# Two more plain column blocks, later sums of squares, and a halved last down projection in a float32 encoder trunk

## The chip, the cores and the metric

The kernel runs on one core of one Trainium2 chip. The metric is the time of one execution on the device in microseconds (us), by the median of several runs. PE is TensorE, DVE is VectorE, ACT is ScalarE, POOL is GpSimd, SP is SyncE; PE's weight loads (PEld) run beside its products.

## The reference, cut to what matters

Two layers over x of 512 positions and 1024 channels, in float32. Each layer is attention with a residual addition, then a mixer; the change lies in the mixer:

```python
x = x + jnp.einsum('bsm,md->bsd', y, w_out[l])
h = rmsnorm(x, g_ffn[l])
gate, val = jnp.split(jnp.einsum('bsd,df->bsf', h, w_up[l]), 2, axis=-1)   # 1024 -> 2 x 2816
gate = centred_dwconv(gate, conv_w[l], conv_b[l])                           # width 3 over the positions
x = x + jnp.einsum('bsf,fd->bsd', jax.nn.silu(gate) * val, w_down[l])       # 2816 -> 1024
```

2816 hidden channels are 22 blocks of 128, 1024 channels are 8.

## The kernel before, in words

Everything is held transposed, channels on the partitions and the 512 positions along the free dimension. Every float32 operand is split into a rounded part (hi, by ACT) and a remainder (lo, by DVE), and a product is three PE instructions, hi x hi, hi x lo and lo x hi (`mm3`, L525). Weights come by SP's queue into `wr`, ACT rounds them to `wh`, DVE subtracts to `wl` (`w_load` L434, `w_high` L484, `w_low` L493); three such units can be ready ahead.

**The planner.** The program is written by tracks (Python generators) that offer one operation at a time; `Machine.run` (L261) models when each could start and, for each engine, takes the offer that starts first, or among offers within 0.1 us of it the one with the lowest rank (`RK`, L47). So the ranks and the model fix each engine's order when the program is built. Ranks that matter here: sums of weights 25, half sums of the input 22, weights 36 while a unit is ready ahead and 2 when none is, x additions behind the output projection 8, sums of squares `nsq` 6, additions of the mixer 42, the column chains 50 plus the block's number. All operations are recorded in one helper, so all have line L258 in the profile; the tiles' names tell them apart. PE's own order in the mixer is one track, `ffn` (L1528), which goes through `mixer_order` (L375).

**Into the mixer.** The last products of the output projection (`out_last`, L1202) are added to x by DVE, and for each of the 8 channel blocks ACT writes nf_h = x times the gain, DVE the remainder nf_l (`Norm.add`, L542). `squares` (L553) sums x squared over the blocks (ACT squares to nf_q, DVE adds to nf_sum), `rms` (L569) reduces that on PE to nf_ss and takes the power -1/2 on POOL, `rb_track` (L1229) spreads the result over the partitions (PE rps, ACT rb). The products of the plain columns don't need rb; what is done with their result does.

**Plain columns** (`up_step` L1370). A hidden block's gate and its value are 8 x 3 products of 512 columns each, each into its own PSUM bank, out of five (`FT`, L1367). `chain_f` (L1282) waits for rb, multiplies the gate by it (DVE, tile gp, which frees the bank), convolves (ACT and twice DVE), takes the SiLU (ACT), multiplies by rb (POOL) and by the value (DVE, cv<-cv,up, which frees the other bank); `act_out` splits the result (act, or acth and actl).

**Column pairs** (`pair_step` L1459, `up_pair` L1386). Two hidden blocks at once by Strassen's scheme with seven products of halves: 7 x 4 x 3 products of 256 columns for the two gates, as many for the two values. The input's half sums (`mixer_forms` L1308: ha, hb, hs, ht and the split f, fa, fb, fc) are made once per layer, when rb is there. The weights' sums ws are made for each pair by `w_sums` (L456), four operations that DVE or POOL may do (`either`). What the products give is put together in dp and du by ACT and DVE.

**Down.** `down_step` (L1548) adds a part's hidden blocks up in one bank per output block (3 products of 512 columns for each hidden block), `down_add` (L1565) adds that to x. Hidden blocks come in four parts:

```python
FF_PARTS = ((0, 6), (6, 12), (12, 18), (18, 22))
PLAIN = 4
```

The first four blocks are plain columns, the other 18 are nine pairs. Part 0's columns come first, then the eight down steps (one per output block) of each part, with the next part's columns spread among them. `later` (L1597) starts the next layer's norm behind the fifth step of the last part; in layer two the outputs are written as each output block is done. `_lay_out` (L1612) arranges the weights in memory.

Of the kernel before, what the change touches and what calls it, by code (L numbers as in the profile page):

```python
# [46 lines left out]
RK = {"w": (2, 45, 30), "qkb": (55, 18), "x": 33, "xl": 8, "a": 2, "b": 18, "evac": 49, "qka": 60, "kv": 45,  # L47
      "bn": 2, "nsq": 6, "av": -4, "bv": 4, "ch": 50, "add": 42, "sec": 1, "nxs": 42, "fin": 42, "sum": 25,
      "hf": 22, "wf": 36}
# [252 lines left out]
def kernel(  # L302
# [71 lines left out]

    def mixer_order():  # L375

        ups = [[(f, 1) for f in range(f0, min(f1, PLAIN))] + [(f, 2) for f in range(max(f0, PLAIN), f1, 2)]
               for f0, f1 in FF_PARTS]
        for f, n in ups[0]:
            yield "up", 0, f, n  # L380
        for pi in range(len(FF_PARTS)):
            after = ups[pi + 1] if pi + 1 < len(FF_PARTS) else []
            at = {NK * i // len(after): u for i, u in enumerate(after)}
            for d in range(NK):
                if d in at:
                    yield ("up", pi + 1, *at[d])
                yield "dn", pi, d, 0

    units = []
    for l in range(depth):  # L390
# [10 lines left out]
        for what, pi, f, n in mixer_order():  # L401
            if what == "dn":
                units.append((w_down[pi][l, f], (FF_PARTS[pi][1] - FF_PARTS[pi][0], P), "down"))
# [130 lines left out]
    class Norm:  # L534
# [18 lines left out]
        def squares(self):  # L553
            eng = dve
            for k in range(NK):
# [8 lines left out]
                yield act.activation(sq[:, :S], x_sb[k], AF.Square)  # L564
                yield eng.tensor_tensor(out=self.part, in0=self.part, in1=sq[:, :S], op=ALU.add)
                m.drop("tmp", sq)
# [98 lines left out]
    def layer(l, norm):  # L665
# [576 lines left out]

        BIG = ("keep", "pair")
        mix = {"forms": 14}

# [5 lines left out]
        def act_out(f, ct):  # L1251

            pi = [i for i, (f0, f1) in enumerate(FF_PARTS) if f0 <= f < f1][0]
            yield lambda: bool(act_places(pi))
# [11 lines left out]
            m.drop("tmp", ct)  # L1266
            m.flags.add(f"{lf}act{f}")

        def conv(f, gt, ct):
# [189 lines left out]
        def pair_step(f):  # L1459
# [34 lines left out]
            def value_piece(n, b, pt, ut, fl):  # L1494
# [25 lines left out]
                i = n // 2  # L1520
                if all(("v", q) in gate for q in (2 * i, 2 * i + 1)):
                    m.spawn(RK["ch"] + f, act_out(f + i, gate["cv", i]))
# [5 lines left out]
        def ffn():  # L1528
            steps = list(mixer_order())
            b_st["rb_left"] = PLAIN + 1  # L1530
# [4 lines left out]
            for i, (what, pi, f, n) in enumerate(steps):  # L1535
                if what == "dn":
                    yield from down_step(pi, f)
                elif n == 1:
                    yield from up_step(f)
                else:  # L1540
                    yield from pair_step(f)
# [6 lines left out]
        def down_step(pi, d):  # L1548
            f0, f1 = FF_PARTS[pi]
            m.flags.add(f"{lf}dn{pi}_{d}")  # L1550
# [7 lines left out]
            done_with(w)  # L1558
            m.spawn(RK["add"], down_add(d, tag, bank, acc, pi == len(FF_PARTS) - 1))
            if d == NK - 1:  # L1560
                for f in range(f0, f1):
                    for v in b_st.pop(("act", f))[0]:
                        m.drop(*v)

        def down_add(d, tag, bank, acc, last):  # L1565
            yield dve.tensor_tensor(out=x_sb[d], in0=x_sb[d], in1=acc, op=ALU.add)
            m.drop(tag, bank)
            if last:
                if l + 1 < depth:
                    yield from nxt.add(d)  # L1570
                else:
                    yield sync.dma_start(out_v[:, d], x_sb[d])

# [21 lines left out]
        if l + 1 < depth:  # L1595
            nxt = Norm(l + 1, 0, f"na{l + 1}")
            def later():  # L1597
                yield m.has(f"{lf}rb", f"{lf}dn{len(FF_PARTS) - 1}_{SQ_FROM}")
                m.spawn(RK["nxs"], nxt.squares())
                m.spawn(2, nxt.rms())  # L1600
# [11 lines left out]
def _lay_out(inp):  # L1612
# [24 lines left out]
    w = a["w_down"].reshape(L, NF, P, NK, P)  # L1637
    for i, (f0, f1) in enumerate(FF_PARTS):
        o[f"w_down{i}"] = np.ascontiguousarray(w[:, f0:f1].transpose(0, 3, 2, 1, 4))
    col = lambda v: v.reshape(L, -1, P).transpose(2, 0, 1)  # L1640
# [21 lines left out]
def _build(nc, arrays, depth=DEPTH):  # L1662
    ap = {n: nc.dram_tensor(n, v.shape, F32, kind="ExternalInput").ap() for n, v in arrays.items()}
    out = nc.dram_tensor("outT", (D, S), F32, kind="ExternalOutput").ap()
    with tile.TileContext(nc, schedule_with_timeline_sim=True) as tc:
        kernel(
            tc, ap["xT"], ap["w_first"], ap["w_in"], ap["w_out0"], ap["w_out1"], ap["w_up"],
            tuple(ap[f"w_down{i}"] for i in range(len(FF_PARTS))), ap["col_par"], ap["row_par"],
            ap["rope"], ap["mask"], ap["ident"], out, depth)
# [11 lines left out]
```

## Time and profile before

| | |
|---|---|
| median of 3 runs | 1184.47 us (1183.8 to 1187.16) |
| the profiled execution | 1185.19 us |
| its span, first to last instruction | 1183.1 us |
| mean granted clock of PE | 0.993 |
| busy: PE / PE weight loads / DVE / ACT / POOL | 1163.1 / 1053.0 / 981.9 / 663.2 / 202.3 us |
| moved by DMA | 103.12 MB |

A matmul's recorded length is longer than its share of PE, because products overlap: what a product costs is the distance of starts. DVE's and ACT's instructions overlap a little at their ends as well. Each of the 2 us stretches below shows how much of it an engine was busy and which clock was granted to PE (1.00 is 2.4 GHz, 0.50 is 1.2 GHz).

### The profile page before, as it was taken

The numbers are of one execution on the slowest core, as the hardware profiler recorded it, in microseconds if no ns is written. First come the engines' busy times: TensorE is split into PE (matmuls) and PEld (weight loads), VectorE is DVE, ScalarE is ACT, GpSimd is POOL, SyncE is SP. The second block draws the span as 40 slices with busy tenths as digits, with TensorE's granted clock in tenths as the row PEclk, the third lists the DMA queues.
The fourth block names the chain that finished last, engine by engine and source line by source line (L and its number), as shares of the span: only waits on it lengthen the run. The fifth ranks groups of instructions, "written<-read, shape, count | busy, mean of one in ns | idle before, by whom it ended". The sixth has DMA issues, their size and how long they took to land.

```text
span 1183.1 us, 20177 instructions
## 1 busy us (share of the span) xinstructions
PE 1163.1 (98%) x7796; PEld 1053.0 (89%) x7796; DVE 981.9 (83%) x1797; ACT 663.2 (56%) x1187; POOL 202.3 (17%) x254
## 2 busy tenths in 40 slices
PE   9999999999999999999999989999999999999998
PEld 7999888978999999999889989888789999999997
DVE  6988899779998888887659888898799988888863
ACT  6779766455564454444537876665555544544441
POOL 2433721010100000000042556110111000000000
PEclk9999999989999999999999999999899999999999
DMA  6221111123223322332332121111232223233323
GB/s 233 66 72 55 54 55 36 54 72 107 68 99 112 111 99 99 112 125 71 107 118 73 37 71 37 55 54 54 71 124 61 96 88 112 98 112 103 121 81 116
DMA packets 33343, 103.12 MB, mean 87 GB/s; under 512 B 3936, under 2 KB 4192, under 8 KB 33248
## 3 DMA queue, kind: packets, MB, share of 16 engines
q1 hardware_dynamic: 33248, 101.84, 26.0%
q8 instruction: 61, 1.00, 0.4%
q14 instruction: 34, 0.28, 0.1%
HBM read 99.73 MB, written 2.10 MB: 86 GB/s over the span
## 4 chain that ended last, share of the span: by engine, by line
PE 79%; DVE 13%; ACT 5%; issue 2%; POOL 0%; DMA 0%; SPq 0%; DVEq 0%; ACTq 0%
PE up L258 32%; PE dn L258 20%; PE wo L258 6%; PE pj_bk L258 3%; PE pj_bv L258 2%; PE pj_akq L258 2%; PE pj_bq L258 2%; DVE wl L258 2%; PE yb L258 2%; PE sc_b L258 2%; PE pt_a L258 1%; PE pv_a L258 1%; PE sc_a L258 1%; PE wt_b L258 1%; ACT so_a L258 1%
## 5 line engine op out<-in xcount | busy, mean ns | idle before, releaser
L258 ACT CAST wh<-wr 128x1024 fp32r<-128x1024 f32 (+2 forms) x200 | 177.2, 887 | 158.9 <-PE up L258 41.3
L258 DVE TENSOR_TENSOR wl<-wr,wh 128x1024 fp32r<-128x1024 f32 (+2 forms) x193 | 196.7, 1020 | 62.9 <-ACT wh L258 62.7
L258 ACT CAST wh<-ws 128x1024 fp32r<-128x1024 f32 x72 | 75.4, 1048 | 109.2 <-DVE ws L258 46.1
L258 PE MATMUL up<-fc,wh 128*128 128x256 f32 x576 | 106.4, 285 | 1.8 <-DVE du L258 1.8
L258 PE MATMUL up<-fa,wh 128*128 128x256 f32 x576 | 107.0, 283 | 0.0
L258 PE MATMUL up<-fb,wh 128*128 128x256 f32 x576 | 105.6, 284 | 0.0
L258 PEld LDWEIGHTS up<-fc,wh 128*128 128x128 f32 x576 | 89.4, 191 | 2.6 <-ACT cv L258 2.1
L258 PEld LDWEIGHTS up<-fb,wh 128*128 128x128 f32 x576 | 89.8, 192 | 0.4 <-ACT dp L258 0.2
L258 PEld LDWEIGHTS up<-fa,wh 128*128 128x128 f32 x576 | 89.8, 192 | 0.1
L258 DVE TENSOR_TENSOR wl<-ws,wh 128x1024 fp32r<-128x1024 f32 x72 | 89.5, 1245 | 0.4 <-ACT wh L258 0.2
L258 PE MATMUL dn<-act,wh 128*128 128x512 f32 x288 | 88.9, 390 | 0.0
L258 PE MATMUL up<-fa,wl 128*128 128x256 f32 x288 | 81.7, 284 | 0.0
L258 PE MATMUL up<-fb,wl 128*128 128x256 f32 x288 | 81.5, 283 | 0.0
L258 PE MATMUL up<-fc,wl 128*128 128x256 f32 x288 | 81.4, 283 | 0.0
L258 PE MATMUL dn<-acth,wh 128*128 128x512 f32 x208 | 81.0, 389 | 0.0
L258 PE MATMUL dn<-actl,wh 128*128 128x512 f32 x208 | 81.0, 389 | 0.0
L258 PE MATMUL dn<-acth,wl 128*128 128x512 f32 x208 | 80.9, 389 | 0.0
L258 POOL TENSOR_TENSOR du<-du 128x256 f32<-128x256 f32 x12 | 8.9, 742 | 395.9 <-DVE du L258 395.9
L258 DVE TENSOR_TENSOR x<-x,dn 128x512 f32<-128x512 f32 x64 | 43.7, 682 | 32.8 <-PE dn L258 32.8
L258 DVE SCALAR_TENSOR_TENSOR cv<-gp,cols,cv 128x512 f32<-128x512 f32 x88 | 63.9, 745 | 0.0
L258 PEld LDWEIGHTS dn<-act,wh 128*128 128x128 f32 x288 | 53.3, 188 | 10.4
L258 ACT ACTIVATE e_b<-sc_b,mx_b,rqb 128x512 f32<-128x512 f32 x64 | 49.1, 776 | 14.6 <-DVE mx_b L258 14.6
(269 smaller groups left out, 3452.4 us busy)
## 6 DMA issues: line engine op xcount, KB each, us to landing
wr<-w_up SPq DMA_DIRECT2D x88, 512.0 KB, 4.5
wr<-w_down SPq DMA_DIRECT2D x48, 384.0 KB, 3.1
wr<-w_in SPq DMA_DIRECT2D x28, 512.0 KB, 3.5
wr<-w_out SPq DMA_DIRECT2D x16, 512.0 KB, 3.4
wr<-w_down SPq DMA_DIRECT2D x16, 256.0 KB, 2.6
x<-xT SPq DMA_DIRECT2D x8, 256.0 KB, 5.5
prob_f<-w_first SPq DMA_DIRECT2D x8, 256.0 KB, 5.6
wr<-w_first SPq DMA_DIRECT2D x4, 512.0 KB, 3.6
```

The source lines that it names most:

```text
L258: getattr(self.raw[op.eng], op.name)(*op.args, **op.kw)
```

## The change

Six blocks instead of four are plain columns in both layers, so eight pairs are left. The rank of the sums of squares goes from 6 to 44. In layer two the parts are of 6, 6, 4 and 6 blocks, and the last part goes down two output blocks at a time by the same scheme of seven products of halves: the halves are of the positions, of two hidden blocks and of two output blocks. For it, `act_forms` makes four split tiles for each pair of hidden blocks in place of `act_out`, and `w_sums` and the casts treat the down weights as a pair's. The columns of that last part are spread over the first five of part 2's eight steps (`EARLY`).

```diff
-FF_PARTS = ((0, 6), (6, 12), (12, 18), (18, 22))
-PLAIN = 4
+FF_PARTS = (((0, 6), (6, 12), (12, 18), (18, 22)), ((0, 6), (6, 12), (12, 16), (16, 22)))
+HALVED = ((), (3,))
+EARLY = 5
+PLAIN = 6
...
-      "bn": 2, "nsq": 6, ...
+      "bn": 2, "nsq": 44, ...
...
+            n = NK // 2 if pi in HALVED[l] else NK
+            gap = min(n, EARLY) if pi + 1 in HALVED[l] else n
+            at = {gap * i // len(after): u for i, u in enumerate(after)}
+            for d in range(n):
                 if d in at:
                     yield ("up", pi + 1, *at[d])
-                yield "dn", pi, d, 0
+                yield "dp" if pi in HALVED[l] else "dn", pi, d, 0
...
+            if what == "dp":
+                units.append((tuple(w_down[l][pi][2 * f + i] for i in range(2)), (nf_part, P), "pair"))
+                units.extend([(None, (nf_part, P), "sum"), (None, (nf_part, P), "sum"), (None, (nf_part // 2, P), "rest")])
...
+        def act_forms(f, ct):
...
+            left, right, both = ce[:, LO], ce[:, HI], slice(0, S)
+            a = yield from place(f"fma{l}_{f}")
+            yield from split(a, left, LO, [("B11", LO)])
+            b = yield from place(f"fmb{l}_{f}")
+            yield from split(b, cf[:, both], both, [("B21", LO), ("B22", HI)])
+            yield either(cf[:, HI], cf[:, HI], right, ALU.subtract)
+            yield either(right, right, left, ALU.subtract)
+            yield either(left, cf[:, HI], left, ALU.add)
+            c = yield from place(f"fmc{l}_{f}")
+            yield from split(c, ce[:, both], both, [("T2", LO), ("T1", HI)])
+            yield either(cf[:, LO], cf[:, LO], left, ALU.subtract)
+            d = yield from place(f"fmd{l}_{f}")
+            yield from split(d, cf[:, both], both, [("T4", LO), ("T3", HI)])
...
+                if any(parts[p][0] <= f < parts[p][1] for p in HALVED[l]):
+                    if all(("v", q) in gate for q in range(4)):
+                        m.spawn(RK["ch"] + f, act_forms(f, [gate["cv", q] for q in range(2)]))
...
+        def down_pair(pi, p, last):
...
+            def add(b, x, o, d):
+                yield dve.tensor_tensor(out=x[:, o], in0=x[:, o], in1=b[2][:, LO], op=ALU.add)
...
+            def second(b):
+                yield dve.tensor_tensor(out=ut[:, 0], in0=pt[:, 0], in1=b[2][:, LO], op=ALU.add)
+                yield either(x1[:, HI], x1[:, HI], ut[:, 0], ALU.add)
+                yield either(both, both, ut[:, 0].unsqueeze(1).broadcast_to([P, 2, CW]), ALU.add)
...
+            def fourth(b):
+                yield dve.tensor_tensor(out=ut[:, 1], in0=pt[:, 1], in1=b[2][:, LO], op=ALU.add)
+                yield either(x2[:, HI], x2[:, HI], ut[:, 1], ALU.add)
...
+            yield from product(b0, u0, 0, "B11", True, True)
+            m.spawn(2, keep(b0, 0, "p1"))
+            yield from product(b1, u1, 0, "T1", True, True)
+            m.spawn(2, keep(b1, 1, "p5"))
+            yield from product(b0, u0, nh, "B21", False, True)
+            m.spawn(RK["add"], add(b0, x1, LO, 2 * p))
+            yield from product(b1, u1, nh, "B22", False, True)
+            m.spawn(RK["add"], add(b1, x1, HI, 2 * p))
+            yield from product(b3, u2, 0, "T3", True, True)
+            m.spawn(RK["sec"], fourth(b3))
+            yield from product(b2, u2, nh, "T2", True, True)
+            m.spawn(RK["sec"], second(b2))
+            yield from product(b3, u3, 0, "T4", False, True)
+            m.spawn(RK["add"], add(b3, x2, LO, 2 * p + 1))
```

`product` is as in `up_pair`, with the part's three block pairs in place of the input's four. An output block is written once its three additions are done.

## Rows read from the trace of the kernel before

**Rows 1.** The page of the profile: busy time of each engine with its share of the span and its instructions, and the granted clock of PE in 40 slices (tenths, 9 is 90% or more).

```profile
PE 1163.1 (98%) x7796; PEld 1053.0 (89%) x7796; DVE 981.9 (83%) x1797; ACT 663.2 (56%) x1187; POOL 202.3 (17%) x254
...
PEclk9999999989999999999999999999899999999999
```

**Rows 2.** The chain that ended last, in order of time: start in us, length in us, engine, tile, number of instructions. The first two lines are small groups of the attention stage, 252.55 and 839.45 stand behind the insertion of rps in each layer, the last two are a column pair and the end of layer two.

```profile
219.41 0.79 PE ss_yb L258 x8
222.35 0.89 PE rt_yb L258 x8
252.55 8.67 PE up L258 x38
...
839.45 8.67 PE up L258 x38
...
958.75 20.20 PE up L258 x168
...
1141.31 38.12 PE dn L258 x168
```

**Rows 3.** PE's timeline at the start of the mixer, layer one (233 to 250 us) and layer two (the last line): start, us, operation, output<-inputs, shapes, count, and in brackets the idle time before it with its releaser.

```profile
236.20 0.40 PE L258 MATMUL up<-nf_h,wh 128*128 128x512 f32 x1
...
239.81 0.50 PE L258 MATMUL up<-nf_l,wh 128*128 128x512 f32 x1 [0.30 <-DVE nf_l L258]
...
242.76 0.50 PE L258 MATMUL up<-nf_h,wh 128*128 128x512 f32 x1 [0.95 <-ACT nf_h L258]
...
823.03 0.40 PE L258 MATMUL up<-nf_h,wh 128*128 128x512 f32 x1
```

**Rows 4.** What PE waited for, from the last output products to the first column pair: 226 to 300 us (three lines) and, for nf_l in layer two, 812 to 890 us (the last line). Total us, times, longest.

```profile
PE up L258 <- DVE nf_l L258: 1.2, 4, 0.3
PE up L258 <- ACT nf_h L258: 1.0, 1, 1.0
PE up L258 <- DVE du L258: 0.9, 1, 0.9
...
PE up L258 <- DVE nf_l L258: 1.3, 4, 0.3
```

**Rows 5.** DVE's timeline in the same place, layer one; columns as in rows 3.

```profile
231.36 0.42 DVE L258 TENSOR_TENSOR x<-x,wo 128x256 f32<-128x256 f32 x1 [0.30 <-PE wo L258]
...
238.40 0.69 DVE L258 TENSOR_TENSOR nf_sum<-nf_sum,nf_q 128x512 f32<-128x512 f32 x1
239.00 0.75 DVE L258 SCALAR_TENSOR_TENSOR nf_l<-x,cols,nf_h 128x512 fp32r<-128x512 f32 x1
239.67 0.68 DVE L258 TENSOR_TENSOR nf_sum<-nf_sum,nf_q 128x512 f32<-128x512 f32 x1
...
241.53 0.41 DVE L258 TENSOR_TENSOR x<-x,wo 128x256 f32<-128x256 f32 x1
```

**Rows 6.** Table of stretches of 2 us, layer one: length, busy time of each engine with its instructions, then PE's granted clock, share and rate of the DMA engines.

```profile
242.00:244.00 2.00, 0.90 (x3) 0.54 (x4) 2.00 (x4) 2.00 (x4) 0.00 (x0) 1.00 0.00 0
...
246.00:248.00 2.00, 2.00 (x10) 1.92 (x9) 0.93 (x3) 0.78 (x1) 0.14 (x1) 0.50 0.25 39
...
250.00:252.00 2.00, 2.00 (x9) 1.61 (x9) 0.00 (x0) 0.00 (x0) 0.00 (x0) 0.61 0.67 250
```

**Rows 7.** DVE's timeline further on: the mean square from PE (nf_v), the first use of rb (ha), and the reads that give PSUM banks back (gp is a gate, cv<-cv,up a value).

```profile
247.62 0.16 DVE L258 TENSOR_SCALAR nf_v<-nf_ss 128x4 f32<-128x4 f32 x1 [1.07 <-PE nf_ss L258]
...
253.26 0.75 DVE L258 SCALAR_TENSOR_TENSOR ha<-x,cols,rb 128x512 f32<-128x512 f32 x1 [4.34 <-ACT rb L258]
...
255.60 0.69 DVE L258 TENSOR_TENSOR gp<-up,rb 128x512 f32<-128x512 f32 x1
...
263.66 0.69 DVE L258 TENSOR_TENSOR gp<-up,rb 128x512 f32<-128x512 f32 x1
...
268.20 0.68 DVE L258 TENSOR_TENSOR cv<-cv,up 128x512 f32<-128x512 f32 x1
...
289.10 1.28 DVE L258 TENSOR_TENSOR gp<-up,rb 128x512 f32<-128x512 f32 x2
```

**Rows 8.** DVE's groups by form in two periods of layer two, 1019.61 to 1084.55 us (busy us, mean ns of one | idle before), and two stretches of layer one with the first pairs; columns of these as in rows 6.

```profile
L258 DVE TENSOR_TENSOR wl<-ws,wh 128x1024 fp32r<-128x1024 f32 x9 | 10.9, 1218 | 0.0
L258 DVE SCALAR_TENSOR_TENSOR cv<-gp,cols,cv 128x512 f32<-128x512 f32 x8 | 5.8, 746 | 0.0
L258 DVE TENSOR_TENSOR wl<-wr,wh 128x768 fp32r<-128x768 f32 x6 | 5.7, 954 | 2.5 <-ACT wh L258 2.5
...
L258 DVE TENSOR_TENSOR x<-x,dn 128x512 f32<-128x512 f32 x6 | 4.1, 680 | 0.0
...
L258 DVE TENSOR_TENSOR du<-dp,up 128x256 f32<-128x256 f32 x8 | 3.3, 418 | 2.3 <-PE up L258 2.3
...
310.00:330.55 20.55, 20.54 (x170) 20.30 (x169) 20.43 (x34) 12.90 (x21) 4.14 (x6) 1.00 0.23 76
330.55:338.73 8.18, 8.18 (x38) 6.75 (x38) 8.18 (x14) 3.18 (x5) 0.00 (x0) 1.00 0.45 167
```

**Rows 9.** Timelines of DVE and POOL near the end of layer two; columns as in rows 3. The first line is the last of the eight weight sums of the last column pair, the other two stand beside each other in time.

```profile
1121.04 0.69 DVE L258 TENSOR_TENSOR ws<-wr,wr 128x512 f32<-128x512 f32 x1
...
1140.81 0.68 DVE L258 TENSOR_TENSOR cv<-cv,dp 128x256 f32<-128x256 f32 x1
...
1140.47 0.74 POOL L258 TENSOR_TENSOR du<-du 128x256 f32<-128x256 f32 x1 [35.67 <-DVE du L258]
```

More of the change, by code (lines that the diff above doesn't have):

```diff
@@ L47 @@
 RK = {"w": (2, 45, 30), "qkb": (55, 18), "x": 33, "xl": 8, "a": 2, "b": 18, "evac": 49, "qka": 60, "kv": 45,
-      "bn": 2, "nsq": 6, "av": -4, "bv": 4, "ch": 50, "add": 42, "sec": 1, "nxs": 42, "fin": 42, "sum": 25,
+      "bn": 2, "nsq": 44, "av": -4, "bv": 4, "ch": 50, "add": 42, "sec": 1, "nxs": 42, "fin": 42, "sum": 25,
       "hf": 22, "wf": 36}
@@ L564, in squares @@
                 yield act.activation(sq[:, :S], x_sb[k], AF.Square)
-                yield eng.tensor_tensor(out=self.part, in0=self.part, in1=sq[:, :S], op=ALU.add)
+                yield dve.tensor_tensor(out=self.part, in0=self.part, in1=sq[:, :S], op=ALU.add)
                 m.drop("tmp", sq)
@@ L1243, in layer @@
         BIG = ("keep", "pair")
+        parts = FF_PARTS[l]
         mix = {"forms": 14}
@@ L1251, in act_out @@
         def act_out(f, ct):
-            pi = [i for i, (f0, f1) in enumerate(FF_PARTS) if f0 <= f < f1][0]
+            pi = [i for i, (f0, f1) in enumerate(parts) if f0 <= f < f1][0]
             yield lambda: bool(act_places(pi))
@@ L1267, in act_out, with place, split @@
             m.flags.add(f"{lf}act{f}")
+        def act_forms(f, ct):
+            fm = b_st["fm", f] = {}
+            held = b_st["act", f] = ([], None)
+            b_st["act", f + 1] = ([], None)
+            ce, cf = ct
+            def place(name):
+                yield lambda: bool(act_places(1))
+                if act_places(1)[0] == "big":
+                    tag = max(BIG, key=lambda t: m.cap[t] - m.live[t])
+                    t = new(tag, name)
+                    held[0].append((tag, t))
+                    got = t[:, 0], t[:, 1]
+                else:
+                    got = new("hid0", name + "h"), new("hid1", name + "l")
+                    held[0].extend([("hid0", got[0]), ("hid1", got[1])])
+                return got
+            def split(t, src, o, names):
+                yield act.copy(t[0][:, o], src)
+                yield dve.tensor_tensor(out=t[1][:, o], in0=src, in1=t[0][:, o], op=ALU.subtract)
+                for n, q in names:
+                    fm[n] = (t[0][:, q], t[1][:, q])
+                    m.flags.add(f"{lf}fm{f}{n}")
+            left, right, both = ce[:, LO], ce[:, HI], slice(0, S)
[9 more added lines that the diff above has]
+            yield either(cf[:, LO], cf[:, LO], left, ALU.subtract)
+            m.drop("tmp", ce)
+            d = yield from place(f"fmd{l}_{f}")
+            yield from split(d, cf[:, both], both, [("T4", LO), ("T3", HI)])
+            m.drop("tmp", cf)
         def conv(f, gt, ct):
@@ L1520, in value_piece @@
                 i = n // 2
-                if all(("v", q) in gate for q in (2 * i, 2 * i + 1)):
+                if any(parts[p][0] <= f < parts[p][1] for p in HALVED[l]):
+                    if all(("v", q) in gate for q in range(4)):
+                        m.spawn(RK["ch"] + f, act_forms(f, [gate["cv", q] for q in range(2)]))
+                elif all(("v", q) in gate for q in (2 * i, 2 * i + 1)):
                     m.spawn(RK["ch"] + f, act_out(f + i, gate["cv", i]))
@@ L1528, in ffn @@
         def ffn():
-            steps = list(mixer_order())
+            steps = list(mixer_order(l))
             b_st["rb_left"] = PLAIN + 1
@@ L1537, in ffn @@
                     yield from down_step(pi, f)
+                elif what == "dp":
+                    yield from down_pair(pi, f, pi == len(parts) - 1)
                 elif n == 1:
@@ L1558, in down_step, with part_done @@
             done_with(w)
-            m.spawn(RK["add"], down_add(d, tag, bank, acc, pi == len(FF_PARTS) - 1))
+            m.spawn(RK["add"], down_add(d, tag, bank, acc, pi == len(parts) - 1))
             if d == NK - 1:
-                for f in range(f0, f1):
-                    for v in b_st.pop(("act", f))[0]:
-                        m.drop(*v)
+                part_done(pi)
+        def part_done(pi):
+            for f in range(*parts[pi]):
+                for v in b_st.pop(("act", f))[0]:
+                    m.drop(*v)
         def down_add(d, tag, bank, acc, last):
@@ L1597, in later @@
             def later():
-                yield m.has(f"{lf}rb", f"{lf}dn{len(FF_PARTS) - 1}_{SQ_FROM}")
+                yield m.has(f"{lf}rb", f"{lf}dn{len(parts) - 1}_{SQ_FROM}")
                 m.spawn(RK["nxs"], nxt.squares())
@@ L1637, in _lay_out @@
     w = a["w_down"].reshape(L, NF, P, NK, P)
-    for i, (f0, f1) in enumerate(FF_PARTS):
-        o[f"w_down{i}"] = np.ascontiguousarray(w[:, f0:f1].transpose(0, 3, 2, 1, 4))
+    for l in range(L):
+        for i, (f0, f1) in enumerate(FF_PARTS[l]):
+            f = [*range(f0, f1, 2), *range(f0 + 1, f1, 2)] if i in HALVED[l] else list(range(f0, f1))
+            o[f"w_down{l}_{i}"] = np.ascontiguousarray(w[l, f].transpose(2, 1, 0, 3))
     col = lambda v: v.reshape(L, -1, P).transpose(2, 0, 1)
@@ L1667, in _build @@
             tc, ap["xT"], ap["w_first"], ap["w_in"], ap["w_out0"], ap["w_out1"], ap["w_up"],
-            tuple(ap[f"w_down{i}"] for i in range(len(FF_PARTS))), ap["col_par"], ap["row_par"],
+            tuple(tuple(ap[f"w_down{l}_{i}"] for i in range(len(p))) for l, p in enumerate(FF_PARTS)), ap["col_par"], ap["row_par"],
             ap["rope"], ap["mask"], ap["ident"], out, depth)
```

98 lines of the change are left out of this document (84 added, 14 removed).

## The prediction

> **What bounds the kernel now.** I read the busy times first [rows 1]: TensorE (PE) is busy for 98% of the span, VectorE (DVE) for 83%. The chain of waits then tells in which stretches PE really sets the pace [rows 2]. From the first column pair on it is one run of PE instructions: a pair takes 20.20 us, the last 168 products of 512 columns take 38.12 us. So a product of 512 columns costs 38.12/168 = 0.2269 us, one of 256 costs 20.20/168 = 0.1202 us, and in these stretches only fewer products, or a DVE that falls behind, move the time.
>
> The exception is the head of each mixer. In PE's timeline [rows 3] the reader is to see the first plain column start at 236.20, and then ever wider spaces between its products. The waits [rows 4] say on whom: nf_l from DVE and nf_h from ACT, none longer than 1.0 us. DVE's timeline [rows 5] shows why: between the nf_l that PE needs, DVE adds squares (nf_sum, 0.60 us apart from the next start), and the last two x are added only from 241.53 on. The table of stretches [rows 6] shows a second price: PE is busy 0.90 of 2 us at 242 to 244, and then the granted clock, still 1.00 there, stands at 0.50 in 246 to 248, so it fell from 2.4 to 1.2 GHz, and it rises again only within 250 to 252.
>
> The size of it: between 236.20 and 252.55 PE issues 33 products of 512 columns, the 8 small ones of nf_ss and the 8 of rps. At full speed that is 33 x 0.2269 + 0.79 + 0.89 = 9.2 us (the two small groups by the equal ones of the attention stage [rows 2]); it took 16.35. Loss: 7.2 us. In layer two, 839.45 - 823.03 = 16.42 [rows 2, 3], loss 7.2 us. Together 14.4 us.
>
> **Part 1, the late squares.** Their rank goes from 6 (ahead of the x adds and nf, rank 8) to 44 (behind these and behind the weights, 36). DVE's work up to the last nf_l is then eight x adds, eight nf_l and one weight remainder: 8 x 0.34 + 8 x 0.66 + 1.14 = 9.1 us (starts lie about 0.08 us closer than the durations: 238.40, 239.00, 239.67 for 0.69 and 0.75 us [rows 5]). From the first x add at 231.36 that ends at 240.5. PE wants the last nf_l at 236.20 + 22 x 0.2269 = 241.2. So the waits nearly vanish, and with them the fall of the clock. I leave 0.7 us per layer for a square that slips into a gap: **-13.0 us** (-14.4 to 0).
>
> What is late next: rb, the inverse norm, which every plain column's gate needs. Squares behind the weights end at about 246, as before; from nf_v at 247.62 by POOL's power to rb it took 5.6 us, partly at half clock [rows 7]; I take 251 for the first use of rb instead of 253.26. PE, however, is 7 us ahead of where it was. A plain column keeps two of five banks, gate and value, until DVE reads them; the reads came at 255.60, 263.66, 268.20 and then only at 289.10 [rows 7], since the half sums (rank 22) and the next pair's weights go before the columns (50 and up). With PE ahead, half number eight (counting from 0) starts at 236.20 + 1.7 + 8 x 5.45 = 281.5 and needs the fourth read. Ceiling of the wait: 289.1 - 281.5 = 7.6 us per layer; floor 0. Against the ceiling stand rb 2 us earlier and no pair weights yet (ws, four sums of 0.60 us before 282 that fall away). Nearer to the floor: 1.0 per layer, **+2.0 us** (0 to 15.2).
>
> **Part 2, six plain blocks.** A pair costs 168 x 0.1202 = 20.2 us, the same two blocks plain 96 x 0.2269 = 21.8. One pair less per layer: **+3.2 us**, all on PE. What DVE does for a pair, 21.1 us (below), falls for the same two blocks to 2 x (3 x 0.60 + 2 x 0.66 + 2 x 1.14) = 10.8. So the first pair no longer starts under a DVE with a full backlog; its wait for du, 0.9 us per layer [rows 4], I put at 0.3: **-1.2 us** (-1.8 to 0).
>
> **Part 3, the halved last part of layer two.** Six blocks, four pairs of outputs: 4 x 7 x 3 x 3 = 252 products of 256 columns, 30.3 us, instead of 8 x 6 x 3 = 144 of 512, 32.7. **-2.4 us** on PE. The price is DVE, by starts (the means of rows 8 less 0.08) [rows 8]: for a column pair 6 x 1.14 + 2 x 0.60 weights, 8 x 0.60 sums, 13 of 256 columns at 0.34 (products' sums, value sums, multiplications), 4 x 0.66 for the convolution and 2 x 0.60 for the remainders of the two blocks, in all 21.1 us against PE's 20.2. For a step of four blocks 0.60 + 0.60 against 2.72. For one halved output pair: sums of 384 columns 4 x 0.47 (between 256 and 512), weights 3 x 0.87 + 0.47, additions 7 x 0.34 + 0.60, in all 7.9 us against PE's 7.6. The forms of a block pair: 4 x 0.34 + 0.34 + 3 x 0.60 = 3.5 us instead of 1.2.
>
> The three last column pairs stand close, with 1, 2 and 5 steps behind them instead of 3 or 4. Over these 82.4 us of PE, DVE has 3 x 23.4 + 8 x 1.2 + 5.0 for the first halved weights = 85 us, less about 8 that it works ahead (in the trace the last sum of the next pair starts at 1121.04 [rows 9], as that pair itself begins at 1179.43 - 38.12 - 20.2 = 1121.1 [rows 2]): 93%. That such a load can be hidden is seen at 310 to 339, where DVE is busy for 99 to 100% and PE never idle [rows 8]. After the last column pair DVE has 42 us (4.9 for its values and forms, 5.4 for five steps, 31.7) against PE's 43.9. But the last forms have the lowest rank (70) and a chain ACT, DVE, ACT, and the second product wants the third of four pieces. From nothing (all hidden) to 9 us (DVE's sum by full durations, 15% more than by starts, 48, and 4 us for the chain); nearest to the first pair, where a DVE without pause cost PE 0.9 us [rows 4], and I count three such places, the three kinds of late work (weights, forms, additions): **+3.0 us**.
>
> The sums that either engine may do I count on DVE: while POOL added du, the DVE instruction beside it took 0.68 us, where one of 256 columns takes 0.42 [rows 8, 9]. The Trainium skill, GPSIMD Engine Reference, section Key points, says that the two share their SBUF interfaces when DVE reads two SBUF operands. The trace agrees; if POOL's help were free, the waits of this part would be 0 and the sum 3 us lower.
>
> **The end.** Before, from the last product to the span's end: 1183.1 - (1141.31 + 38.12) = 3.7 us [rows 2], one addition and one output. After, two outputs end together and the second product's additions are still running: 2 x 0.34 + 0.60 begins 1.08 us before the last product ends. **+0.4 us** (0 to 1).
>
> Sum, against the profiled execution's 1185.19 us (span 1183.1): -13.0 + 2.0 + 3.2 - 1.2 - 2.4 + 3.0 + 0.4 = -8.0, so 1177.2. The median of the runs, 1184.47, lies 0.7 lower; **forecast 1176.5 us**.
>
> **Rivals.** *A, as summed*, chance 0.62. Its own range: with all waits gone 1169, with its costs half way to their ceilings 1181.
>
> *B, the plain columns run out of banks.* Place: the fifth plain column's gate. If DVE's fourth read comes later than PE by 3.6 us or more, that is again a hole like that of 242 to 244, and about 6 us at half clock follow [rows 6], 3.0 us lost. Per layer 3.6 - 1.0 + 3.0 = 5.6: 1176.5 + 11 = 1188; at the ceiling, with 7.6 for 3.6, 1196. It decides from 3.6 us on. For it: the times of the reads [rows 7]. Against: rb earlier, no sums in between. 0.13.
>
> *C, DVE sets the pace in the tail.* The close column pairs and the halved outputs cost 11 us of waits instead of 3, half clock for a while included: 1184.5. For it: 21.1 against 20.2 and 7.9 against 7.6. Against: the full DVE that held nothing up [rows 8]. 0.15. The clock's fall weighs here: it came after waits of at most 1.0 us each [rows 4, 6]. The Trainium skill, TensorE: Matmul & The Clock Gate, section Why this matters for your kernels, asks for a long idle gap between bursts. By the page C would lose its waits alone and end 3 us sooner; the trace does not agree with it.
>
> *D, the late squares do not do what they say.* The planner takes what can start first, and squares fill every gap of ACT and DVE. Then the 14.4 us stay, and so does PE's delay (no bank wait): 1185.2 + 3.2 - 1.2 - 2.4 + 3.4 - 0.7 = 1187.5. Against: DVE is without a gap from 238.40 on [rows 5]. 0.10.
>
> **How the numbers follow.** About 0.3%, 3.6 us, is what a measurement of this kernel can tell: faster is below 1180.9, slower above 1188.0. A gives 0.60 of faster and the rest same; C gives 0.05 of faster, the rest same; D is mostly same; B slower with some of D. Faster 0.65, same 0.20, slower 0.15. Range: A from its lowest, C and D whole, 1169 to 1188; outside are most of B and the rim of D.
>
> **What would show it.** Right: no wait of PE for nf_l or nf_h, granted clock 1.00 throughout both heads, the first pair about 68 us after the first plain column in each layer (65.4 of products and 1.7 small), in layer two 252 products of 256 columns at the end. Wrong: a wait of the fourth to sixth plain column for DVE's gp (B), waits for wl, or for forms on ACT or DVE, in the last 115 us (C), nf_sum still between the nf_l (D). If the sum comes out below 1169, some DVE work that I call hidden was on PE's path already before.

## The result and the profile after

The changed kernel takes 1178.14 us (median of 5 runs, 1177.27 to 1179.02), the kernel before 1183.8 us in the same runs: ratio 0.9949 [0.9932, 0.9966]. The profiled execution took 1178.77 us with a span of 1177.0, so 6.1 us of span less than before. Where they went, by starts of instructions in the two traces: the mixer of layer one (first product of `up` to the first `pj_akq` of the next layer) fell from 591.64 - 236.20 = 355.44 us to 587.58 - 236.65 = 350.93, so by 4.51; that of layer two (to its last product) from 1179.02 - 823.03 = 355.99 to 1172.73 - 819.41 = 353.32, so by 2.67. The end takes 0.2 us longer, and the stretches in front of the two mixers, which the change does not touch, 0.9 us. Executions also differ outside the mixers: in the attention of layer two the granted clock stands at 0.50 for up to 6.8 us in some of the profiled executions below and not at all in others, and that attention takes between 229.6 and 232.8 us, so the mixers' times are read beside the medians.

The page of the changed kernel; it answers to [rows 1]. PE has lost 5.8 us of busy time, DVE has gained 14, and PE's clock is at 0.9 or more in every slice.

```profile
PE 1157.3 (98%) x7760; PEld 1046.7 (89%) x7760; DVE 996.0 (85%) x1818; ACT 664.3 (56%) x1191; POOL 204.5 (17%) x259
...
PEclk9999999999999999999999999999999999999999
```

PE's timeline in the head of the mixer, layer one, and the first product of layer two (as [rows 3]):

```profile
236.65 0.40 PE L260 MATMUL up<-nf_h,wh 128*128 128x512 f32 x1
...
242.13 0.50 PE L260 MATMUL up<-nf_l,wh 128*128 128x512 f32 x1 [0.87 <-DVE nf_l L260]
...
249.12 1.05 PE L260 MATMUL nf_ss<-unit,nf_sum 128*128 128x1 f32 x8
250.03 0.48 PE L260 MATMUL up<-nf_h,wh 128*128 128x512 f32 x1
...
252.43 1.16 PE L260 MATMUL rps<-ident,nf_r 128*128 128x128 f32 x8
253.34 0.48 PE L260 MATMUL up<-nf_h,wh 128*128 128x512 f32 x1
...
819.41 0.40 PE L260 MATMUL up<-nf_h,wh 128*128 128x512 f32 x1
```

From 236.65 to the product behind rps at 253.34, PE now issues 57 products where it issued 33 before. The stretch is 16.69 us long against 252.31 - 236.20 = 16.11 before, so 24 x 0.2269 - 0.58 = 4.9 us are won per layer. The one long wait left is for the seventh of the eight nf_l. The waits that the view names for PE between 226 and 310 us (as [rows 4]; neither DVE's du nor a bank is in it):

```profile
PE up L260 <- DVE nf_l L260: 0.9, 1, 0.9
PE wo L260 <- DVE x L260: 0.2, 1, 0.2
```

DVE's timeline shows the order that did it (as [rows 5, 7]): no nf_sum before the last nf_l, but two weight remainders in front of the last two nf_l, of which 240.19 is one. Behind them come nf_v, the first use of rb (ha), and the reads that give the plain columns' banks back.

```profile
239.53 0.75 DVE L260 TENSOR_TENSOR x<-x,wo 128x256 f32<-128x256 f32 x2
240.19 1.22 DVE L260 TENSOR_TENSOR wl<-wr,wh 128x1024 fp32r<-128x1024 f32 x1
241.33 1.41 DVE L260 SCALAR_TENSOR_TENSOR nf_l<-x,cols,nf_h 128x512 fp32r<-128x512 f32 x2
242.65 2.28 DVE L260 TENSOR_TENSOR nf_sum<-nf_sum,nf_q 128x512 f32<-128x512 f32 x3
...
245.99 3.08 DVE L260 TENSOR_TENSOR nf_sum<-nf_sum,nf_q 128x512 f32<-128x512 f32 x4
250.21 0.16 DVE L260 TENSOR_SCALAR nf_v<-nf_ss 128x4 f32<-128x4 f32 x1 [1.15 <-PE nf_ss L260]
...
254.24 0.75 DVE L260 SCALAR_TENSOR_TENSOR ha<-x,cols,rb 128x512 f32<-128x512 f32 x1 [2.73 <-ACT rb L260]
...
256.58 1.29 DVE L260 TENSOR_TENSOR gp<-up,rb 128x512 f32<-128x512 f32 x2
...
271.87 0.68 DVE L260 TENSOR_TENSOR cv<-cv,up 128x512 f32<-128x512 f32 x1
```

Two waits too short for the list stand in front of the small products. nf_ss starts at 249.12, when DVE's last nf_sum ended at 249.06, and rps at 252.43, when POOL's nf_r ended at 252.38; each comes about 0.25 us late. POOL's timeline:

```profile
250.45 1.93 POOL L260 TENSOR_TENSOR nf_r<-nf_v,unit 128x4 f32<-128x4 f32 x1 [28.51 <-DVE nf_v L260]
```

The stretches of [rows 6]: PE is busy 1.87 of 2 us where it was 0.90, and the clock stays at 1.00, 2.4 GHz.

```profile
242.00:244.00 2.00, 1.87 (x8) 1.52 (x9) 1.90 (x4) 0.95 (x2) 0.00 (x0) 1.00 0.72 223
246.00:248.00 2.00, 2.00 (x11) 1.65 (x10) 1.79 (x4) 0.56 (x2) 0.00 (x0) 1.00 0.47 104
```

In layer two a part of it is given back. PE's waits between 1080 and 1175 us, where the kernel before had one unbroken run of products [rows 2]:

```profile
PE dn L260 <- DVE du L260: 1.1, 3, 0.7
PE up L260 <- DVE wl L260: 0.8, 1, 0.8
PE up L260 <- DVE du L260: 0.4, 2, 0.2
PE up L260 <- ACT wh L260: 0.2, 1, 0.2
```

A wait also shifts the products around it, so the rows undercount: measured against the steady distance of starts, products come late by 2.1 us in the three close column pairs (0.33 at 1087.14, 0.40 at 1106.03, 1.02 at 1107.29, 0.38 at 1114.73) and by 2.1 us at the halved outputs (0.88 at 1147.39, 0.37 at 1155.64 and 1163.89, three times 0.16).

### The profile page after: what moved, and what is told of

It reads as the page before. It is cut to its first block, busy times and chain, and to the rows that moved or that the text cites. A ratio compares the mean times of both kernels' runs of the same rounds, so it can differ in the third digit from the quotient of the medians.

```text
span 1177.0 us, 20150 instructions
## 1 busy us (share of the span) xinstructions
PE 1157.3 (98%) x7760; PEld 1046.7 (89%) x7760; DVE 996.0 (85%) x1818; ACT 664.3 (56%) x1191; POOL 204.5 (17%) x259
## 4 chain that ended last, share of the span: by engine, by line
PE 70%; DVE 17%; issue 7%; ACT 4%; POOL 1%; DMA 1%; SPq 0%; DVEq 0%; ACTq 0%; POOLq 0%
PE up L260 27%; PE dn L260 17%; PE wo L260 5%; DVE wl L260 4%; PE pj_bk L260 3%; PE pj_akq L260 3%; PE pj_bv L260 2%; PE pj_bq L260 2%; DVE ws L260 2%; PE yb L260 2%; PE sc_b L260 2%; DVE cv L260 1%; PE pt_a L260 1%; PE wt_b L260 1%; PE pv_a L260 1%
## 5 line engine op out<-in xcount | busy, mean ns | idle before, releaser
L260 DVE TENSOR_TENSOR wl<-wr,wh 128x1024 fp32r<-128x1024 f32 (+3 forms) x193 | 200.0, 1037 | 63.1 <-ACT wh L260 62.7
L260 ACT CAST wh<-ws 128x1024 fp32r<-128x1024 f32 (+1 forms) x72 | 73.5, 1024 | 106.6 <-PE dn L260 37.3
L260 PE MATMUL up<-fc,wh 128*128 128x256 f32 x512 | 94.3, 284 | 0.4 <-DVE du L260 0.4
L260 DVE TENSOR_TENSOR wl<-ws,wh 128x1024 fp32r<-128x1024 f32 (+1 forms) x72 | 86.8, 1211 | 0.0
L260 PE MATMUL up<-nf_l,wh 128*128 128x512 f32 x192 | 75.0, 391 | 1.7 <-DVE nf_l L260 1.7
L260 PE MATMUL up<-nf_h,wh 128*128 128x512 f32 x192 | 75.3, 392 | 0.0
L260 PE MATMUL up<-nf_h,wl 128*128 128x512 f32 x192 | 74.8, 389 | 0.0
L260 PE MATMUL dn<-acth,wh 128*128 128x512 f32 x176 | 68.6, 390 | 0.0
L260 PE MATMUL dn<-actl,wh 128*128 128x512 f32 x176 | 68.6, 390 | 0.0
L260 PE MATMUL dn<-acth,wl 128*128 128x512 f32 x176 | 68.5, 389 | 0.0
```

What stands on the lines that cost most here:

```text
L260: getattr(self.raw[op.eng], op.name)(*op.args, **op.kw)
```

## The experiments

**First question: which part of the change brings the gain?** The change has three parts. Four kernels leave one out or make one alone.

*e1: the changed kernel with early squares.*

```diff
-"nsq": 44
+"nsq": 6
```

> The changed kernel with the rank of the sums of squares back at 6. Theory: the gain is the late squares', about 5 us of head loss per layer (7.2 before, 2.3 after), so it comes out near 1188 us, with nf_sum between the nf_l again, PE waiting for nf_l and nf_h, and the granted clock at 0.50 for some 6 us in both heads. Rival (the six plain blocks give the gain, since DVE has more time for what is late): it stays within 3 us of the changed kernel, 1178 to 1181.

*e2: the kernel before with late squares alone.*

```diff
-"nsq": 6
+"nsq": 44
```

> The kernel before with the rank 44 alone, four plain blocks and no halves. Theory, if the terms add up: minus 5 us per layer, about 1174 us, PE waits for the first pair's du at most 1 us per layer as before. Rival (the gain needs the six plain blocks): PE now reaches the first pair 5 us sooner while DVE has as much to do until then, so most of the gain is given back in waits for DVE at the first pair, 3 to 5 us per layer there, and the time is 1180 to 1184.

*e3: the changed kernel without the halves.*

```diff
-FF_PARTS = (((0, 6), (6, 12), (12, 18), (18, 22)), ((0, 6), (6, 12), (12, 16), (16, 22)))
-HALVED = ((), (3,))
+FF_PARTS = (((0, 6), (6, 12), (12, 18), (18, 22)), ((0, 6), (6, 12), (12, 18), (18, 22)))
+HALVED = ((), ())
```

> The changed kernel without the halved last part: layer two has the parts of layer one. Theory: the halves cost more than the 2.4 us that PE saves (waits for DVE in the last 100 us of about 4 us, 0.3 us at the end), so it is 2 us faster than the changed kernel, about 1176 us, and PE doesn't wait in the second mixer behind its head. Rival (the halves pay, and the waits would be there without them because of the six plain blocks): 1178.5 to 1181.

*e4: the kernel before with six plain blocks alone.*

```diff
-PLAIN = 4
+PLAIN = 6
```

> The kernel before with six plain blocks alone, squares at rank 6, no halves. Theory: 1.6 us more of products per layer, less 0.9 us of wait at the first pair: about 1185 us, head loss of 7 us per layer and half clock as before. Rival (more plain blocks by themselves relieve DVE): 1179 to 1181.

Measured, with the mixer of layer one, in which nothing is halved, beside the whole:

| kernel | squares | plain blocks | halves | mixer of layer one, us | median, us | ratio to the kernel before |
|---|---|---|---|---|---|---|
| before | early | 4 | no | 355.44 | 1184.76 beside e1 to e4 | 1 |
| e4 | early | 6 | no | 355.61 | 1185.4 | 1.0004 [0.999, 1.0017] |
| e2 | late | 4 | no | 360.04 | 1191.88 | 1.0059 [1.0046, 1.0072] |
| e1 | early | 6 | yes | 355.54 | 1187.17 | 1.0022 [1.0013, 1.0031] |
| e3 | late | 6 | no | 350.93 | 1175.76 | 0.9922 [0.991, 0.9934] |
| after | late | 6 | yes | 350.93 | 1178.14 | 0.9949 [0.9932, 0.9966] |

Neither half of the gain exists alone. Six plain blocks alone change nothing, late squares alone cost 4.6 us in layer one, and the two together save 4.5. By the medians the halves cost (e1 against e4, the changed kernel against e3), but the intervals of both pairs overlap; the third question takes that from the traces. The early squares of e1 bring the old head back, with the clock down to 1.2 GHz:

```profile
242.00:244.00 2.00, 1.30 (x4) 0.78 (x4) 2.00 (x5) 1.97 (x4) 0.00 (x0) 0.89 0.00 0
246.00:248.00 2.00, 2.00 (x8) 1.86 (x9) 0.92 (x3) 0.39 (x1) 0.53 (x1) 0.50 0.34 98
```

PE's timeline of the same head shows rps with its input ready in time (POOL ends nf_r at 249.39): the group starts 0.22 us behind the product in front of it, so without the delay of the changed kernel.

```profile
250.52 0.39 PE L260 MATMUL up<-nf_h,wl 128*128 128x512 f32 x1
250.74 1.05 PE L260 MATMUL rps<-ident,nf_r 128*128 128x128 f32 x8
```

e2 is longer than either of its forecasts. Why late squares alone lose is seen where the first column pair begins. In the kernel before it starts at 288.48 us, and the last piece of the input's half sums (fc) starts on DVE at 286.10: 2.4 us ahead. PE's and DVE's timelines of the kernel before:

```profile
288.48 0.40 PE L258 MATMUL up<-f,wh 128*128 128x256 f32 x2
```

```profile
286.10 0.68 DVE L258 TENSOR_TENSOR fc<-ht,fc 128x512 fp32r<-128x512 f32 x1
```

In e2 PE comes 4.7 us sooner, at 283.75, while DVE is only then making the fourth block's ha, and fc follows at 291.72. So the half sums also come 5.6 us later than before: from 236 us on DVE has put seven weight sums, nine weight remainders and four gates ahead of that fc, where it had put four, eight and two. PE's and DVE's timelines of e2:

```profile
283.75 0.40 PE L258 MATMUL up<-f,wh 128*128 128x256 f32 x2
...
286.13 0.38 PE L258 MATMUL up<-f,wh 128*128 128x256 f32 x1 [1.15 <-ACT f L258]
...
291.57 0.80 PE L258 MATMUL up<-fb,wh 128*128 128x256 f32 x2 [1.40 <-ACT dp L258]
```

```profile
284.10 0.74 DVE L258 SCALAR_TENSOR_TENSOR ha<-x,cols,rb 128x512 f32<-128x512 f32 x1
...
291.72 0.68 DVE L258 TENSOR_TENSOR fc<-ht,fc 128x512 fp32r<-128x512 f32 x1
```

Its stretches show DVE without a pause, PE in pieces, and the clock at 0.50 afterwards. The first two pairs take 51.2 us, where they took 41.9:

```profile
284.00:286.00 2.00, 0.98 (x9) 0.77 (x7) 2.00 (x4) 1.79 (x3) 1.08 (x1) 1.00 0.00 0
...
290.00:292.00 2.00, 0.60 (x3) 0.43 (x3) 2.00 (x5) 1.16 (x3) 0.13 (x2) 0.50 0.00 0
292.00:294.00 2.00, 2.00 (x11) 2.00 (x11) 1.00 (x2) 0.00 (x0) 0.00 (x0) 0.50 0.00 0
```

In e3 the two further plain blocks put the pair at 305.97, with fc at 289.15. The time for DVE that they give, not a cheaper product, is what they are worth. To test that reading, *e8* takes load from DVE there, in `mixer_forms` of e2 (it leaves a subtraction out), and keeps four plain blocks:

```diff
 def split(t, src, o):
     yield act.copy(t[:, 0, o], src)
-    yield dve.tensor_tensor(out=t[:, 1, o], in0=src, in1=t[:, 0, o], op=ALU.subtract)
+    yield act.copy(t[:, 1, o], src)
```

> The kernel before with the sums of squares made late alone (four plain column blocks; 1191.9 us), but the low remainders of the input's half sums are written by ScalarE as copies, not by VectorE as differences: the subtraction is left out, so the values differ. Theory (with only four plain blocks TensorE reaches the first pair before VectorE has made the half sums of the input): the waits at 282 to 292 us shrink, 1176 to 1183 us. Rival (the loss comes from the clock or from the late sums themselves): it stays at 1188 to 1192 us.

1178.31 us, ratio 0.9954 [0.9938, 0.9971]; mixer of layer one 587.07 - 236.31 = 350.76 us. The pair starts at 283.70 as in e2, and PE runs through it at full clock:

```profile
284.00:286.00 2.00, 2.00 (x19) 2.00 (x19) 2.00 (x4) 1.62 (x3) 0.00 (x0) 1.00 0.00 0
```

So the late half sums were what stopped PE in e2, as expected; the rival (the clock, or the late sums themselves) falls: the sums of squares are as late here as in e2, and four plain blocks then do as well in layer one as six (350.93). How much of e2's loss the clock added, once the waits had brought it down, is not separated.

**Second question: do the plain columns come near their banks?** *e9* takes a place away in e3.

```diff
-FT = ("mm", "at", "sc")
+FT = ("mm", "sc")
```

> The changed kernel without the halves (1175.8 us), but the plain columns share four banks of PSUM instead of six. The rival of the banks said that plain columns past the fourth are stopped by banks; the reads of the held halves were seen 4 to 10 us ahead of the need with six banks. With two banks fewer each plain half needs the read two halves sooner (about 5 to 6 us): if that is the margin, 1 to 1.5 us of waits in each layer, about 1178 us; if the banks are far from the limit, unchanged, 1175 to 1176.5 us; if the margin was misread and the reads are the limit, over 1182 us.

This text counts wrongly: the plain columns have five places (mm 2, at 1, sc 2), and e9 leaves four. 1176.74 us, ratio 0.9927 [0.9912, 0.9941], the same as e3; between 236 and 300 us PE's only listed wait is that for the seventh nf_l. The twelve plain halves end at 305.62, at 5.446 us each, so half 8 (counting from 0) starts at 283.8 and half 9 at 289.3. With four places half 8 needs the fifth read and half 9 the sixth; e9's DVE timeline has them in time by 0.7 and 0.4 us:

```profile
282.44 0.68 DVE L260 TENSOR_TENSOR gp<-up,rb 128x512 f32<-128x512 f32 x1
...
288.19 0.67 DVE L260 TENSOR_TENSOR cv<-cv,up 128x512 f32<-128x512 f32 x1
```

With five places each half needs one read less, so the changed kernel has about 6 us to spare and more.

**Third question: what do the halves lose, and why?** Between the changed kernel and e3, layer two's mixer differs by 353.32 - 350.67 = 2.65 us, although PE has 2.4 us less to do, so some 5 us of waits are to be explained; 4.2 of them are the late products above. The trace at the first halved output, DVE and then PE, shows one place: the fourth product (T4) goes on in a bank that DVE's du must have read, and a weight remainder stands ahead of that du.

```profile
1145.96 0.95 DVE L260 TENSOR_TENSOR wl<-wr,wh 128x768 fp32r<-128x768 f32 x1
1146.83 0.42 DVE L260 TENSOR_TENSOR du<-dp,dn 128x256 f32<-128x256 f32 x1
```

```profile
1147.39 0.36 PE L260 MATMUL dn<-fmd_16h,wh 128*128 128x256 f32 x1 [0.72 <-DVE du L260]
```

*e5* takes the remainders of the halved weights from DVE (in `w_low`; ACT copies the weights, and the subtraction is left out); *e6* leaves DVE's work as it is and changes the order of the products (in `down_pair`).

```diff
+            elif kind in ("pair", "sum", "rest") and k in (6, 3):
+                yield act.copy(lo, raw)
             else:
                 yield dve.tensor_tensor(out=lo, in0=raw, in1=hi, op=ALU.subtract)
```

> The changed kernel (1178.1 us), but the low remainders of the halved down weights of layer two (the units with 6 or 3 row blocks) are written by ScalarE as a copy of the raw weights, not by VectorE as a difference: the subtraction is left out, so the values differ. VectorE loses about 3 us of work per pair of output blocks. Theory (VectorE is full in the halved stretch, 2.9 to 3.0 of every 3 us, and its weight remainders stand ahead of the du sums, which TensorE waits for): most of the waits of 2.5 to 3 us go, 1175 to 1176.5 us. Rival (the waits come from the order: the sum for the fourth product is made only one product before it is needed, however free VectorE is): 1177.5 to 1178.5 us.

```diff
             m.spawn(RK["add"], add(b0, x1, LO, 2 * p))
-            yield m.has(fl + "p5")
-            yield from product(b1, u1, nh, "B22", False, True)
-            done_with(u1)
-            m.spawn(RK["add"], add(b1, x1, HI, 2 * p))
             yield unit_there
             u2 = next_unit()
             yield roomy(DT)
             b3 = bank(3)
             yield from product(b3, u2, 0, "T3", True, True)
             m.spawn(RK["sec"], fourth(b3))
+            yield m.has(fl + "p5")
+            yield from product(b1, u1, nh, "B22", False, True)
+            done_with(u1)
+            m.spawn(RK["add"], add(b1, x1, HI, 2 * p))
```

> The changed kernel (1178.1 us) with the seven half products taken in another order, the third product (T3) moved between B11's and B22's parts, so that the sum for the fourth product has one product (1.3 us and more) longer to be made. Order theory: the waits at the fourth product (about 0.9 us in one pair of blocks, 1.6 to 2 us over three) vanish, about 1176.5 us. Load theory (VectorE is full, so a later need only shifts which sum or remainder is late): 1177.5 us or more.

e5: 1176.9 us, 0.9941 [0.9924, 0.9957]. e6: 1175.89 us, 0.9933 [0.9916, 0.995]. The intervals overlap with each other and with the changed kernel's; the traces tell more. Layer two's mixer takes 352.20 us in e5 and 351.04 in e6, against 353.32. (Layer one's, which is the same in the changed kernel, e3, e5, e6, e7 and e11, takes 350.93 to 351.30 us, so 0.4 us tells nothing.) In both, no product waits for du behind 1135 us. One stretch of the changed kernel, of e6 and of e5, in this order:

```profile
1140.00:1148.00 8.00, 7.28 (x60) 7.06 (x59) 7.90 (x15) 3.76 (x6) 0.00 (x0) 1.00 0.30 94
```

```profile
1140.00:1148.00 8.00, 8.00 (x69) 8.00 (x68) 7.83 (x16) 3.91 (x7) 0.00 (x0) 1.00 0.26 75
```

```profile
1140.00:1148.00 8.00, 7.92 (x66) 7.71 (x65) 5.58 (x12) 6.51 (x11) 0.00 (x0) 1.00 0.49 144
```

In e5 DVE is busy 5.58 of 8 us and the waits for du go; three products come 0.24 us late in their place, and a wait for ACT's wh at 1103.76, ahead of the halved stretch, is 0.8 us long (0.2 in the changed kernel, 0.6 in e6). In e6 DVE is as good as full, 7.83 of 8 us against 7.90 in the changed kernel, and PE never stops. So it was the order on a full DVE, not the load alone: with a product more between a sum and its use, the same work fits. The load theory's figure for e6, 1177.5 or more, is not met by the median, though one of e6's six executions reaches it; e5's own figure, 1175 to 1176.5, is missed by 0.4.

What stays are the late products in the three close pairs, 2.4 us in e6, about what PE saves by the halves: e6 and e3 differ by 0.4 us in layer two's mixer. Two kernels ask whether the closeness makes them. *e7* (from the changed kernel) and *e11* (from e6) take the last pairs at steps 0, 2, 5 and 0, 2, 4 instead of 0, 1, 3.

```diff
-EARLY = 5
+EARLY = 8      # e7;  e11: EARLY = 6
```

> The changed kernel (1178.1 us) with the last part's columns of layer two taken earlier between the pairs (at steps 0, 2 and 5), so that the pairs with seven half products do not stand as close together ahead of the halved stretch. If the bunching of pairs makes the waits of 2.1 us between 1087 and 1115 us, these go: about 1176 us. If the halved stretch itself, which then follows the last forms by fewer steps, sets the cost: 1178 to 1180 us, with new waits at its start.

> The kernel with the third product moved sooner (0.9933 of the kernel before), with the last columns of layer two at steps 0, 2 and 4 in place of 0, 1 and 3. If three pairs close together make the waits of 2 us at 1085 to 1114 us, these shrink: about 1174.5 us. If VectorE's whole load of that stretch makes them, they only move, and the last forms come one step nearer to the halved stretch: unchanged to 1 us longer, 1175.5 to 1177 us.

e7: 1186.11 us, 1.0017 [1.0006, 1.0029], longer than either theory had it. e11: 1176.67 us, 0.9931 [0.9916, 0.9946]; its layer two mixer takes 352.10 us, 1.1 more than e6's, and the late products of its last pairs add up to 3.3 us. Spreading does not help, so the closeness is not the cause. What is left is DVE: from 1084 to 1116 us it is busy 31.96 of 32 us in the changed kernel and 31.27 in e11, but 26.94 in e3, where PE is busy all 32. No kernel with the halves takes load off DVE in that stretch, so this cause is argued and not shown.

e7 also shows the price of the last forms. They follow the last pair by three steps, and PE stands still until ACT has written fmc, for which ACT had waited 4.1 us for DVE's cv. The lines are of PE's and ACT's timelines and the stretches behind it:

```profile
1147.26 0.39 PE L260 MATMUL dn<-fmc,wh 128*128 128x256 f32 x1 [4.51 <-ACT fmc L260]
```

```profile
1146.59 0.62 ACT L260 CAST fmc<-cv 128x512 fp32r<-128x512 f32 x1 [4.14 <-DVE cv L260]
```

```profile
1143.00:1147.00 4.00, 0.00 (x0) 0.00 (x0) 3.52 (x8) 0.41 (x1) 0.00 (x0) 1.00 0.00 2
1147.00:1150.00 3.00, 2.40 (x10) 2.21 (x11) 1.72 (x3) 1.09 (x3) 0.00 (x0) 0.60 0.00 0
```

With four steps (e11) and five (the changed kernel) there is no wait for a form.

*e10* halves the last part of layer one as well, on top of e6.

```diff
-FF_PARTS = (((0, 6), (6, 12), (12, 18), (18, 22)), ((0, 6), (6, 12), (12, 16), (16, 22)))
-HALVED = ((), (3,))
+FF_PARTS = (((0, 6), (6, 12), (12, 16), (16, 22)), ((0, 6), (6, 12), (12, 16), (16, 22)))
+HALVED = ((3,), (3,))
```

> The kernel with the third product moved sooner (0.9933 of the kernel before), with the last six blocks of the first layer halved as well. If the seven products cost no waits when their order is right, the first layer gains what the second did against the kernel without halves, 1 to 2.4 us: about 1174 us, ratio 0.992. If the squares of the next norm, which VectorE makes beside that stretch in the first layer only, collide with the sums of the halves, the first layer loses 1 to 4 us: 1177 to 1180 us, with waits for du sums between 540 and 592 us.

1179.25 us, 0.9948 [0.9933, 0.9963]: slower than e9 and e11 on the same chip, by medians of 2.5 us, though the intervals overlap. Layer one's mixer takes 588.63 - 236.22 = 352.41 us against 350.93, and 351.30 in e6. The second theory named the size, but not the place: PE's waits between 430 and 600 us are those of the pairs again, and only 0.5 us of them lie in the halved stretch.

```profile
PE up L260 <- ACT wh L260: 0.8, 1, 0.8
PE up L260 <- DVE wl L260: 0.8, 1, 0.8
PE dn L260 <- DVE wl L260: 0.5, 1, 0.5
PE up L260 <- DVE du L260: 0.2, 1, 0.2
```

The changed kernel has no wait there. Layer two's program is that of e6, yet its mixer takes 352.34 us against 351.04: behind two waits of 0.78 and 0.75 us in the close pairs (at 1105.50 and 1106.76) the granted clock fell to 0.50 for 3.4 us. A stretch of it:

```profile
1108.00:1110.00 2.00, 2.00 (x11) 2.00 (x11) 2.00 (x5) 0.37 (x1) 0.00 (x0) 0.50 0.00 0
```

The best version is e3: 0.9922 against 0.9949 for the whole change. They ran on different chips and their intervals just touch; the 2.65 us in the trace of layer two's mixer speak for it too. e6 with its 0.9933 cannot be told from e3.

## Why the prediction was right, point by point

The forecast of 1176.5 us stands 1.6 below the result, and the case is the one called A. Not each step held, and that the sum came so near is in part luck: the late squares brought 3.3 us less than forecast and the halves cost 2.1 more, while two terms that were to cost 2.0 each cost nothing and 0.3.

| step | forecast, us | measured, us | by |
|---|---|---|---|
| late squares, both heads | -13.0 | -9.7 | starts in the heads, 2 x 4.87 |
| plain columns' banks | +2.0 | 0 | no wait; e9 |
| six plain blocks, du of the first pair | +2.0 | +0.3 | e4, layer one's 0.17 twice |
| halves on PE, and their waits | -2.4 + 3.0 | +2.65 | changed kernel against e3 |
| the end | +0.4 | +0.2 | last product to the span's end |
| stretches in front of the mixers | 0 | +0.9 | first products of the mixers |
| not accounted for | | -0.4 | |
| span | -8.0 | -6.1 | |

- **The late squares were sized too high.** The mechanism was as forecast: no nf_sum ahead of nf_l, no fall of the clock. But 2.1 us per head stay. 1.1 of it is the seventh nf_l: two weight remainders (235.75 and 240.19) went ahead of it where I counted one. Another 0.5 is the two small groups, which come 0.25 us late each, for the last nf_sum and for nf_r; in e1, where nf_r was ready, there is no such delay at rps. The rest is spread in steps of about 0.1 us: the groups themselves, and the second product behind a break (250.34 instead of 250.26). I had booked all of that as loss that goes.
- **The bank wait was put at 1 us per layer and is none**, although rb came later (ha at 254.24, not 251). The ceiling took the fourth read at 289.10 [rows 7] as it was; it came at 271.87, since no pair's sums and weights stood before it. I had named that against the ceiling and taken too little off for it.
- **The sum of parts 1 and 2 hid a condition.** I added them as if each were there alone. e2 and e4 show that they are not: the early squares' 4.9 us per head were slack for the half sums, of which PE could have taken back 2.4 us before it ran into them (fc at 286.10, the pair at 288.48), and with PE ahead the half sums themselves come 5.6 us later (e2). The prediction saw that the first pair starts under a DVE with less backlog, and priced that at 0.6 us per layer. Alone, without the two further blocks, late squares would have been worth +4.6 us per layer and not -6.5. Of the rivals none had this mechanism.
- **The halves** cost the waits I feared in kind (a DVE without slack), and more of them: 5.0 us against 3.0. Of the three places, weights (1.4 us at the close pairs, and 0.7 for du there) and additions (2.1 us at T4) were there; forms were not, and e7 shows how near they are. "93%" for DVE over the close pairs was too low an average: between 1084 and 1116 us it is full.
- **Rival B** falls with e9, by its margin. **Rival D** falls with the order on DVE. **Rival C** is right about the engine, by the argument above, and wrong in the size: 5 us instead of 11. The clock stays at 1.00 through these waits in the changed kernel's trace; that it can fall there, e10 shows. As for the Trainium skill, TensorE: Matmul & The Clock Gate, section Why this matters for your kernels, which asks for a long idle gap: the one wait of 4.5 us in e7 was followed by 0.60, which agrees; e2's fall at 288 us came behind waits of at most 1.15 us each, which does not.

## What to carry to other kernels

A stall ahead of a stage can be the slack of the next one: before removing it, look up when the next stage's inputs are ready and by how much (here 2.4 us of 4.9, and the inputs then came 5.6 us later too), and remove it together with the work that gives the inputs time. An algorithm that saves products (2.4 us here) did not pay where the vector engine, which makes its sums, was full; putting another product between a sum and its use won 2.3 us of the 2.65 back (e6), more than lightening the load did (e5, 1.1). Price parts of a change singly and in pairs: here the single prices were +0.2 and +4.6 us per layer, and the pair's -4.5.

## What the runs showed of the hardware that was not expected

- The clock does not fall behind every wait, and the waits alone do not decide it. Behind one wait of 0.87 us (242.13, changed kernel) the granted clock stayed at 1.00; behind two of 1.15 and 0.46 us close together (e2, 285 to 287 us) it went to 0.50, and behind one of 4.5 us (e7) to 0.50 as well, a mean of 0.60 over the next 3 us. Behind two waits of 0.78 and 0.76 us, 1.3 us apart, it stayed at 1.00 in e5 (1103.76 and 1105.02), and behind two of 0.78 and 0.75 us, as far apart, it fell in e10.
- Eight small products in a run of products of 512 columns hardly cost more than themselves when their input is ready: in e1 rps took 0.81 us by starts, without a delay in front, and the second product behind it came 0.09 us late.
- Taking the remainders of the input's half sums from DVE (e8) was worth 1.05% of the whole by the ratios of e2 and e8 (1.0059 and 0.9954), some 12 us (by the traces 9.3 us in layer one's mixer and 8.5 in layer two's): they lay on the path to the first pairs, and the waits for them took the clock with them.
